# Sample attention with its partitions ordered (batch, quarter, token), and its transfers on SyncE's queue

## The chip, the core and the metric

The kernel runs on one core of a Trainium2 chip. The metric is device time in microseconds (us) of one execution, the median of several runs. Before the change the median of three runs is 2064.51 us (2064.17 to 2070.43). One more execution was taken by the hardware profiler.

## What is computed

One layer of a decoder trunk, for a prompt of 256 tokens and for 8 sample sequences of 4 tokens that share the weights: 288 token columns in all, everything in fp32. Cut to what matters here:

```
h = RMSNorm(x)                                    # d_model 2048
qa,ka,va,za,ba,aa, qb,kb,vb, uc, ga,gb,gc = split(h @ w_in)
out_a = gated delta rule over qa,ka,va            # 8 heads, prompt in chunks
out_b = dilated attention over qb,kb,vb           # 3 groups x 4 heads x 128
oc    = multi-scale pooling of uc, then w_pool
merged = sigmoid(ga)*(out_a@w_br_a) + sigmoid(gb)*(out_b@w_br_b) + sigmoid(gc)*(oc@w_br_c)
x = x + RMSNorm(merged @ w_out)
x = x + RMSNorm(SwiGLU(RMSNorm(x)))

# dilated attention of one sample token, group g with (window, dilation) = (128,1), (512,4), (2048,16)
idx = q_idx - arange(window // dil + 1) * dil     # rows of cache_win{g+1} followed by the 4 new rows
s   = q . k[idx] / sqrt(128);  p = exp(s - max)   # the max and the sum run over all three groups
out_b = sum(p * v[idx]) / sum(p)
```

The sample group reads its old keys and values from `cache_win1` (8 x 128 rows), `cache_win2` (8 x 512) and `cache_win3` (8 x 1024). One row is a key and a value of 4 heads x 128 numbers, 2 KB each. The new keys and values are also outputs (`win*_prompt`, `win*_sample`), and the kept part of the caches is copied to `win*_sample`.

## The kernel before, in words

**The trunk.** All large matmuls run through one list of items (`run_items`, L229). A weight tile is 128 x 1024 numbers, 512 KB. `load` (L158) brings it into one of five `raw` buffers on SyncE's queue, called SP here (L169). `feed` (L172) turns it into two fp32r parts: ScalarE (ACT) casts it to `wh` (L180), VectorE (DVE) computes the rest `wl` (L184). There are three buffers of each, and `feed(3)` keeps three tiles ready. Then TensorE (PE) runs 24 matmuls for the tile, 128 x 128 times 128 x 288 (L253 to L255). A `raw` buffer is free for the next load when L184 has read it. After each weight tile, `step` (L282) lets the background generators go on; their rates say how many of their pieces go with one tile.

**Where the keys and values are born.** Nine items compute qb, kb and vb of the three groups. The last evacuation of each (`evac_qkv`, L955) transposes the result on PE, copies it to `nat` tiles (L979, L981), and stores these by DMA: prompt rows to `win*_prompt` (L986), sample rows to a scratch array `scr` in DRAM (L988) and to `win*_sample` (L991). The `nat` tiles, like most others, come from a ring of 98 slots that is used in turn, so a later user of a slot waits for the store that reads it.

**Sample attention** (`attn_sample`, L1077) runs as a generator at 4.4 pieces a weight tile, started after the second key item and drained when branch b begins (`attn_finish`, L1009). It uses no matmul for the scores. A cache row for all sequences at once is a tile `kr` of 128 partitions x 512 numbers, 256 KB. For groups 2 and 3 the 128 partitions are 8 sequences x 4 quarters of the window x 4 tokens, and the kernel before orders them (token, batch, quarter). Each token needs other rows of the cache, since the dilation is 4 or 16: `sources` (L1101) writes the cache row as a pattern with the 4 tokens `r` outermost, then the 32 pairs (b q) (L1104 to L1106). There are 32 such rows of group 2 and 16 of group 3, for keys and again for values: 96 loads at L1106. For group 1 the partitions are (batch, 16 pieces of the window), one dimension of 128, 8 rows for keys and 8 for values (L1111); there the four tokens are handled by four instructions for each head. The new rows come from `scr` (`by_t`, L1086, and L1112).

For each row and head DVE does one instruction of 128 x 128 (four for group 1): a product with the query and a sum for the scores (L1142), then in the second pass a multiply-add into the output (L1192). Between the passes the maximum over partitions goes through DRAM in small DMAs (L1155 to L1167), and at the end PE adds over partitions with the 0/1 matrices `sel1` and `sel0` (L1196).

**Order of the work.** All DMAs of sample attention and of `evac_qkv` are issued by GpSimd (POOL; `dq` and `self.dq`), whose instructions run in order: a load that waits for a free `kr` buffer holds what is behind it. There are five `kr` buffers (`KR`, L25). Four loads are issued at the start (L1132), and each row that is taken up issues one more before it (L1123), so the load of the fourth row ahead uses the buffer of the row just finished. The first sample instruction after a new weight tile is tied behind that tile's L184 (`paced`, L274). The compiler framework orders the instructions of each engine by a model of their times, within the dependencies of the program; only the cache copies (L165) keep the written order.

Of the kernel before, what the change touches and what calls it, by code (L numbers as in the profile page):

```python
# [9 lines left out]
F32 = mybir.dt.float32  # L10
# [7 lines left out]
NT, NP, NS = 288, 256, 32  # L18
# [6 lines left out]
KR = 5  # L25
EPS = 1e-6
SC = 128.0 ** -0.5
WIN = (128, 512, 1028)
# [11 lines left out]
def shape_constants():  # L40
    r = np.arange(128)
    t, i = r[:, None], r[None, :]
    same4 = t // 4 == i // 4
    d = {}
    d["ident"] = t == i
    d["U"] = t <= i
    d["V"] = t > i
    d["ones"] = np.ones((128, 128))
    d["Ub"] = (t <= i) & same4
    d["Vb"] = (t > i) & same4  # L50
    d["m32"] = (i // 32 == t // 32 + 1) & ((t // 32) % 2 == 0)
    d["m64"] = (t < 64) & (i >= 64)
    d["mS1"] = same4 & (t % 2 == 0) & (i == t + 1)
    d["mS2"] = same4 & (t % 4 < 2) & (i % 4 >= 2)
    d["blk"] = t // 32 == np.arange(4)[None]
    d["bm"] = (t % 32) // 4 == np.arange(8)[None]
    d["bsel"] = t // 4 == np.arange(32)[None]
    c = np.arange(32)[None]
    d["sel1"] = (t // 32 == c % 4) & ((t % 32) // 4 == c // 4)
    d["sel0"] = np.concatenate([(t // 16 == c // 4) & (c % 4 == tt) for tt in range(4)], axis=1)  # L60
    d["fold"] = t % 32 == i % 32
    d["gsel"] = t % 32 == np.arange(16)[None]
    s0 = t % 16
    m0 = np.zeros((128, 4, 9), bool)
    for tt in range(4):
        m0[:, tt, :8] = s0 * 8 + np.arange(8)[None] >= tt
        m0[:, tt, 8] = ((s0 % 4 == 0) & (s0 // 4 <= tt))[:, 0]
    d["mask0"] = np.where(m0, 0.0, -1e30).reshape(128, 36)
    mt = np.ones((128, 50), bool)
    mt[:, 48:] = t % 4 == 0  # L70
    d["maskt"] = np.where(mt, 0.0, -1e30)
    ic = np.zeros((4, 15))
    for gi, w in enumerate((2, 4, 8, 16)):
        ic[gi] = 1.0 / np.minimum(w, np.arange(15) + 1)
    d["icnt"] = np.broadcast_to(ic.reshape(1, 60), (128, 60))
    for qb, name in ((0, "mp0"), (1, "mp1")):
        parts = []
        for dil in DILS:
            for kb in range(qb + 1):
                dist = (qb * 128 + t) - (kb * 128 + i)  # L80
                ok = (dist >= 0) & (dist % dil == 0) & (dist <= 128 * dil)
                parts.append(np.where(ok, 0.0, -1e30))
        d[name] = np.concatenate(parts, axis=1)
    pack = lambda spec: np.ascontiguousarray(
        np.concatenate([np.asarray(d[n], np.float32) for n, _ in spec], axis=1))
    return pack(C_SPEC), pack(M_SPEC)


class Layer:
# [865 lines left out]
    def evac_qkv(self, kind, g):  # L955
        vT = []

        def evac(h, ps):
            nc = self.nc
            t = self.res.popleft()  # L960
            nc.scalar.copy(t, ps)
            if kind == 2:
                vT.append(t)
            else:
                (self.kT if kind == 1 else self.qT)[g, h] = t
            if h < 3:
                return
            src = vT if kind == 2 else [(self.kT if kind == 1 else self.qT)[g, j] for j in range(4)]
            for tb in ([2] if kind == 0 else [1, 2] if (kind == 1 and g == 0) else [0, 1, 2]):
                w = NS if tb == 2 else 128  # L970
                p = self.ps("knat")
                for j in range(4):
                    nc.tensor.transpose(p[:w, j * 128:j * 128 + 128], src[j][:, tb * 128:tb * 128 + w],
                                        self.c["ident"])
                for hp in range(2):
                    n = self.U(name="nat")
                    cs = slice(hp * 256, hp * 256 + 256)
                    if hp == 0:
                        nc.scalar.copy(n[:w, :256], p[:w, cs])  # L979
                    else:  # L980
                        nc.vector.tensor_copy(n[:w, :256], p[:w, cs])  # L981
                    if tb < 2:
                        if not (g == 0 and tb == 0):
                            o = self.o[f"win{g + 1}_prompt"][0, 0].rearrange("r k h d -> r k (h d)")
                            r0 = 0 if g == 0 else tb * 128
                            self.dq.dma_start(o[r0:r0 + 128, kind - 1, cs], n[:, :256])  # L986
                    else:
                        self.dq.dma_start(self.scr[kind, g][:, cs], n[:NS, :256])  # L988
                        if kind > 0:
                            o = self.o[f"win{g + 1}_sample"][0].rearrange("b r k h d -> b r k (h d)")  # L990
                            self.dq.dma_start(o[:, WIN[g] - 4:, kind - 1, cs], n[:NS, :256])  # L991
                    if kind == 2 and tb < 2:
                        self.vn[g, tb, hp] = n
                    else:
                        self.free(n)
            self.free(*vT)
        evac.res = 4
        return evac
# [78 lines left out]
    def attn_sample(self, pool):  # L1077
        nc, c, a, scr = self.nc, self.c, self.a, self.scr
        dq = nc.gpsimd
        qt = pool.tile([128, 2, 512], F32, name="qt")  # L1080
        big = pool.tile([128, 4, 512], F32, name="big")
# [4 lines left out]
        def by_t(dst, kind, g):  # L1086
            src = scr[kind, g].rearrange("(b t) d -> t b d", t=4)
            for t in range(4):
                dq.dma_start(dst[t * 32:t * 32 + 32], src[t][:, None, :].to_broadcast([8, 4, 512]))

        for g in (1, 2):
            by_t(qt[:, g - 1], 0, g)
        q0s = scr[0, 0].rearrange("(b t) d -> t b d", t=4)
        for t in range(4):
            dq.dma_start(big[:, t], q0s[t][:, None, :].to_broadcast([8, 16, 512]))
        cw = [a["cache_win1"][0], a["cache_win2"][0], a["cache_win3"][0]]

        def row():
# [2 lines left out]
        def sources(kv):  # L1101

            for g, dil, n in ((1, 4, 32), (2, 16, 16)):
                src = cw[g].rearrange("b (q m r) k h d -> m k r (b q) (h d)", q=4, r=dil)  # L1104
                for m in range(n):
                    yield g, (m if g == 1 else 32 + m), lambda kr, s=src[m, kv][:4]: dq.dma_start(kr, s)  # L1106
            for g in (1, 2):
                yield g, 47 + g, lambda kr, g=g: by_t(kr, 1 + kv, g)
            src = cw[0].rearrange("b (s m) k h d -> m k (b s) (h d)", m=8)
            for m in range(8):  # L1110
                yield 0, m, lambda kr, s=src[m, kv]: dq.dma_start(kr, s)  # L1111
            yield 0, 8, lambda kr: dq.dma_start(kr, scr[1 + kv, 0][:, None, :].to_broadcast([32, 4, 512]))  # L1112

        todo = deque((kv,) + r for kv in range(2) for r in sources(kv))
        got = deque()

        def load():
            kv, g, m, fill = todo.popleft()
            kr = row()
            fill(kr)  # L1120
            got.append((kv, g, m, kr))
# [7 lines left out]
                if not got:  # L1129
                    return  # L1130

        for _ in range(KR - 1):  # L1132
            load()
        yield 5

        for g, m, kr in rows(0):
            for h in range(4):
                hs = slice(h * 128, h * 128 + 128)
                for t in (range(4) if g == 0 else (0,)):
                    q = big[:, t, hs] if g == 0 else qt[:, g - 1, hs]  # L1140
# [7 lines left out]
        mt = pool.tile([128, 4], F32, name="mt")  # L1148
        m0 = pool.tile([128, 16], F32, name="m0")
        nc.vector.tensor_reduce(mt, sct, axis=AX, op=OP.max)  # L1150
        nc.vector.tensor_reduce(m0, sc0.rearrange("p t h m -> p (t h) m"), axis=AX, op=OP.max)
        dmt = self.dr.tile([32, 16], F32, name="dmt")
        dm0 = self.dr.tile([8, 16, 4, 4], F32, name="dm0")
        dmx = self.dr.tile([4, 8, 4], F32, name="dmx")
        dq.dma_start(dmt.rearrange("c (q h) -> (c q) h", h=4), mt)  # L1155
        dq.dma_start(dm0.rearrange("b s t h -> (b s) (t h)"), m0)
        gm = pool.tile([32, 80], F32, name="gm")
        dq.dma_start(gm[:, 0:16], dmt)
# [2 lines left out]
        yield 4  # L1161
        mx = pool.tile([32, 4], F32, name="mx")
        self.paced(nc.vector.tensor_reduce(mx, gm.rearrange("p (x h) -> p h x", h=4), axis=AX, op=OP.max))
        dq.dma_start(dmx.rearrange("t b h -> (t b) h"), mx)
        dq.dma_start(mt, dmx.rearrange("t b h -> (t b) h")[:, None, :].to_broadcast([32, 4, 4]))
        for t in range(4):
            dq.dma_start(m0[:, t * 4:t * 4 + 4], dmx[t][:, None, :].to_broadcast([8, 16, 4]))  # L1167
        yield 4
        self.paced(nc.vector.tensor_tensor(sct, sct, mt[:, :, None].to_broadcast([128, 4, 50]), op=OP.subtract))
        s0 = sc0.rearrange("p t h m -> p (t h) m")  # L1170
# [9 lines left out]
        for g, m, kr in rows(1):  # L1180
            for h in range(4):
                hs = slice(h * 128, h * 128 + 128)
                for t in (range(4) if g == 0 else (0,)):
                    dst = o0[:, t, hs] if g == 0 else ot[:, hs]
# [336 lines left out]
```

## Time and profile before

| What | Value |
|---|---|
| median of 3 runs | 2064.51 us |
| the profiled execution | 2068.37 us, its span in the profile 2066.6 us |
| PE busy | 2010.6 us, 97% of the span, 15212 matmuls |
| DVE busy | 1324.2 us, 64% |
| ACT busy | 893.8 us, 43% |
| POOL busy | 291.6 us, 14% |
| moved by DMA | 425.50 MB: SP's queue (q1) 384.72 MB, POOL's (q0) 37.73 MB |
| sample attention's scores | DVE instructions from 451.4 to 742.9 us |
| sample attention's values | DVE instructions from 775.9 to 1051.3 us |

How to read it: PE's busy time is the union of modelled matmul times, so the idle time is what counts. A row `A <- B: total, times, longest` in the view of waits says how long A's engine sat idle until B released it. In the view by stretches of time each engine has its busy time with its instructions in brackets, then come the clock granted to PE (1.00 is full speed), the mean busy share of the 16 DMA engines, and the GB/s moved. The DMA share counts a packet from its start to its end, its waits on the way included. "DMA to landing" is the time from the issue of a transfer until its last byte is reported.

### The profile page before, as it was taken

The page shows a single profiled execution, that of the slowest core. Times are in us where ns is not written, and L with a number is a line of the kernel's source. Part 1 is how long each engine was busy: PE and PEld are TensorE (multiplying, and loading weights), DVE is VectorE, ACT ScalarE, POOL GpSimd, SP SyncE. Part 2 cuts the span into 40 slices and gives each one's busy share as a digit, 9 for nine tenths or more (in the row PEclk, how much of TensorE's full clock was granted, in tenths as well). Part 3 has the DMA queues.
Part 4 walks back from the last instruction along what each step waited for, and adds up shares of the span by engine and source line. Part 5 has one row for each costly group of instructions (what it writes and reads, how often), then busy time and mean ns, then how long its engine had stood idle before and what let it go on. Part 6 is the DMA issues. An engine that isn't in the chain of part 4 may idle for free. (4 is left out here: it accounts for less than half of the span.)

```text
span 2066.6 us, 38707 instructions
## 1 busy us (share of the span) xinstructions
PE 2010.6 (97%) x15212; PEld 1984.4 (96%) x15212; DVE 1324.2 (64%) x2857; ACT 893.8 (43%) x1414; POOL 291.6 (14%) x504
## 2 busy tenths in 40 slices
PE   8999999999799999989999989999999999999998
PEld 8989998999799999989999989999999999999997
DVE  7969558567688779878875475543554445454555
ACT  6654473453344444333334454334333333333344
POOL 2326312523320022322000000000000000000001
PEclk9999999999999999999999989999999999999999
DMA  8565546959995668998677646766767767677662
GB/s 268 160 182 169 176 140 197 228 173 238 219 205 183 181 184 198 226 220 245 195 229 234 218 160 212 226 222 217 225 216 228 230 217 226 218 225 227 217 205 97
DMA packets 240310, 425.50 MB, mean 206 GB/s; under 512 B 42736, under 2 KB 83200, under 8 KB 238464
## 3 DMA queue, kind: packets, MB, share of 16 engines
q1 hardware_dynamic: 207712, 384.72, 63.1%
q0 software_dynamic: 32272, 37.73, 8.0%
q8 instruction: 119, 1.95, 0.4%
q10 hardware_dynamic: 144, 0.59, 0.1%
q14 instruction: 63, 0.52, 0.1%
HBM read 410.44 MB, written 66.63 MB: 231 GB/s over the span
## 5 line engine op out<-in xcount | busy, mean ns | idle before, releaser
L184 DVE TENSOR_TENSOR wl<-raw,wh 128x1024 fp32r<-128x1024 f32 x585 | 720.2, 1232 | 519.0 <-ACT wh L180 516.7
L180 ACT CAST wh<-raw 128x1024 fp32r<-128x1024 f32 x585 | 612.7, 1050 | 917.9 <-PE m L254 792.3
L253 PE MATMUL m<-hh,wh 128*128 128x288 f32 x1792 | 532.7, 299 | 4.2 <-ACT wh L180 3.7
L255 PE MATMUL m<-hh,wl 128*128 128x288 f32 x1792 | 524.0, 298 | 8.3 <-DVE wl L184 8.3
L254 PE MATMUL m<-hl,wh 128*128 128x288 f32 x1792 | 531.3, 298 | 0.0
L253 PE MATMUL m<-xgh,wh 128*128 128x288 f32 x1408 | 415.8, 297 | 4.0 <-ACT xgh L373 4.0
L254 PE MATMUL m<-xgl,wh 128*128 128x288 f32 x1408 | 415.8, 296 | 3.2 <-DVE xgl L374 3.2
L255 PE MATMUL m<-xgh,wl 128*128 128x288 f32 x1408 | 414.6, 296 | 0.0
L255 PEld LDWEIGHTS m<-hh,wl 128*128 128x128 f32 x1792 | 335.1, 189 | 13.1 <-DVE wl L184 10.7
L253 PEld LDWEIGHTS m<-hh,wh 128*128 128x128 f32 x1792 | 337.7, 189 | 7.8 <-ACT wh L180 4.2
L254 PEld LDWEIGHTS m<-hl,wh 128*128 128x128 f32 x1792 | 338.2, 189 | 1.9 <-issue 1.8
L253 PEld LDWEIGHTS m<-xgh,wh 128*128 128x128 f32 x1408 | 265.5, 189 | 4.6 <-ACT xgh L373 4.3
L254 PEld LDWEIGHTS m<-xgl,wh 128*128 128x128 f32 x1408 | 266.4, 189 | 3.6 <-DVE xgl L374 3.5
L255 PEld LDWEIGHTS m<-xgh,wl 128*128 128x128 f32 x1408 | 265.4, 189 | 0.0
L253 PE MATMUL m<-hidh,wh 128*128 128x288 f32 x704 | 207.5, 295 | 0.0
L254 PE MATMUL m<-hidl,wh 128*128 128x288 f32 x704 | 207.2, 295 | 0.0
L255 PE MATMUL m<-hidh,wl 128*128 128x288 f32 x704 | 206.5, 295 | 0.0
L1449 POOL TENSOR_TENSOR yo<-y,xr 128x288 f32<-128x288 f32 x7 | 5.6, 821 | 1060.7 <-DVE y L1440 1060.7
L254 PEld LDWEIGHTS m<-hidl,wh 128*128 128x128 f32 x704 | 132.4, 188 | 0.0
L253 PEld LDWEIGHTS m<-hidh,wh 128*128 128x128 f32 x704 | 132.2, 188 | 0.0
L255 PEld LDWEIGHTS m<-hidh,wl 128*128 128x128 f32 x704 | 131.9, 188 | 0.0
L1106 POOL DMA_DIRECT2D kr<-cache_win x96 | 65.4, 682 | 250.0 <-DVE junk L1142 136.9
(386 smaller groups left out, 2704.4 us busy)
## 6 DMA issues: line engine op xcount, KB each, us to landing
raw<-w_in SPq DMA_DIRECT2D x247, 512.0 KB, 4.5
raw<-w_gu SPq DMA_DIRECT2D x176, 512.0 KB, 4.0
raw<-w_down SPq DMA_DIRECT2D x88, 512.0 KB, 4.9
win_sample<-cache_win SPq DMA_DIRECT2D x64, 512.0 KB, 5.4
kr<-cache_win POOLq DMA_DIRECT2D x112, 256.0 KB, 10.7
raw<-w_out SPq DMA_DIRECT2D x32, 512.0 KB, 5.0
win_sample<-cache_win SPq DMA_DIRECT2D x32, 508.0 KB, 5.2
st<-state_gdn SPq DMA_DIRECT2D x64, 128.0 KB, 3.2
```

The costliest lines, as they stand in the source:

```text
L180: i = nc.scalar.copy(wh, raw)
L184: self.last_wl = nc.vector.tensor_tensor(wl, raw, wh.bitcast(F32), op=OP.subtract)
L253: nc.tensor.matmul(out, lhsT=wh[:, c], rhs=xh, start=k == 0, stop=False)
L254: nc.tensor.matmul(out, lhsT=wh[:, c], rhs=xl, start=False, stop=False)
L255: nc.tensor.matmul(out, lhsT=wl[:, c], rhs=xh, start=False, stop=k == nk - 1)
L1106: yield g, (m if g == 1 else 32 + m), lambda kr, s=src[m, kv][:4]: dq.dma_start(kr, s)
L1449: (nc.vector if how == "v" else nc.gpsimd).tensor_tensor(out[:, d % 2], y, x, op=OP.add)
```

## The change

1. Partitions of groups 2 and 3 are ordered (batch, quarter, token). The pattern of a cache row becomes (b q) outermost with 32, then the 4 tokens; the stored constants `sel1` and `maskt` follow, and a DMA for one token writes every fourth partition (`t:128:4`) where it wrote a block of 32.
2. `evac_qkv`'s stores, `by_t`, the queries and all rows are issued by SyncE.
3. `KR - 2` loads are issued at the start, so that rows are loaded three ahead; there are still five buffers.
4. In the exchange of the maximum, the DRAM array is ordered (batch, token), and one DMA for `mt` becomes four.

```diff
-    d["sel1"] = (t // 32 == c % 4) & ((t % 32) // 4 == c // 4)
+    d["sel1"] = (t // 16 == c // 4) & (t % 4 == c % 4)
...
-    mt[:, 48:] = t % 4 == 0
+    mt[:, 48:] = (t // 4) % 4 == 0
@@ evac_qkv @@
-                            self.dq.dma_start(o[r0:r0 + 128, kind - 1, cs], n[:, :256])
+                            nc.sync.dma_start(o[r0:r0 + 128, kind - 1, cs], n[:, :256])
...
-                        self.dq.dma_start(self.scr[kind, g][:, cs], n[:NS, :256])
+                        nc.sync.dma_start(self.scr[kind, g][:, cs], n[:NS, :256])
...
-                            self.dq.dma_start(o[:, WIN[g] - 4:, kind - 1, cs], n[:NS, :256])
+                            nc.sync.dma_start(o[:, WIN[g] - 4:, kind - 1, cs], n[:NS, :256])
@@ attn_sample @@
-                dq.dma_start(dst[t * 32:t * 32 + 32], src[t][:, None, :].to_broadcast([8, 4, 512]))
+                nc.sync.dma_start(dst[t:128:4], src[t][:, None, :].to_broadcast([8, 4, 512]))
...
-            dq.dma_start(big[:, t], q0s[t][:, None, :].to_broadcast([8, 16, 512]))
+            nc.sync.dma_start(big[:, t], q0s[t][:, None, :].to_broadcast([8, 16, 512]))
...
-                src = cw[g].rearrange("b (q m r) k h d -> m k r (b q) (h d)", q=4, r=dil)
+                src = cw[g].rearrange("b (q m r) k h d -> m k (b q) r (h d)", q=4, r=dil)
                 for m in range(n):
-                    yield g, (m if g == 1 else 32 + m), lambda kr, s=src[m, kv][:4]: dq.dma_start(kr, s)
+                    yield g, (m if g == 1 else 32 + m), lambda kr, s=src[m, kv][:, :4]: nc.sync.dma_start(kr, s)
...
-                yield 0, m, lambda kr, s=src[m, kv]: dq.dma_start(kr, s)
-            yield 0, 8, lambda kr: dq.dma_start(kr, scr[1 + kv, 0][:, None, :].to_broadcast([32, 4, 512]))
+                yield 0, m, lambda kr, s=src[m, kv]: nc.sync.dma_start(kr, s)
+            yield 0, 8, lambda kr: nc.sync.dma_start(kr, scr[1 + kv, 0][:, None, :].to_broadcast([32, 4, 512]))
...
-        for _ in range(KR - 1):
+        for _ in range(KR - 2):
             load()
...
-        dmx = self.dr.tile([4, 8, 4], F32, name="dmx")
-        dq.dma_start(dmt.rearrange("c (q h) -> (c q) h", h=4), mt)
+        dmx = self.dr.tile([8, 4, 4], F32, name="dmx")
+        dq.dma_start(dmt.rearrange("(t b) (q h) -> b q t h", t=4, h=4), mt)
...
-        dq.dma_start(dmx.rearrange("t b h -> (t b) h"), mx)
-        dq.dma_start(mt, dmx.rearrange("t b h -> (t b) h")[:, None, :].to_broadcast([32, 4, 4]))
+        dq.dma_start(dmx.rearrange("b t h -> t b h"), mx)
         for t in range(4):
-            dq.dma_start(m0[:, t * 4:t * 4 + 4], dmx[t][:, None, :].to_broadcast([8, 16, 4]))
+            dq.dma_start(mt[t:128:4], dmx[:, t][:, None, :].to_broadcast([8, 4, 4]))
+            dq.dma_start(m0[:, t * 4:t * 4 + 4], dmx[:, t][:, None, :].to_broadcast([8, 16, 4]))
```

## The prediction, made before the changed kernel was run

> **What bounds the kernel now.** I read the page, then PE's busy time by stages of sample attention, then PE's waits in the stages that have idle time, then the transfers there.
>
> ```profile
> PE 2010.6 (97%) x15212; PEld 1984.4 (96%) x15212; DVE 1324.2 (64%) x2857; ACT 893.8 (43%) x1414; POOL 291.6 (14%) x504
> ```
>
> PE is the bound: a change of the transfers can only win back idle time of PE, or add some. The stages follow the DVE instructions that use the rows: group 2 and 3 rows of keys, group 1 rows of keys, the exchange of the maximum, then the same for values. The columns are the stretch, its length, five engines, PE's clock, the DMA share and GB/s.
>
> ```profile
> 450.00:628.00 178.00, 164.97 (x1231) 162.85 (x1230) 131.22 (x497) 71.31 (x109) 55.47 (x91) 0.98 0.99 225
> 628.00:743.00 115.00, 115.00 (x871) 114.69 (x870) 93.25 (x354) 48.24 (x65) 7.66 (x17) 1.00 0.59 175
> 743.00:775.00 32.00, 30.33 (x229) 30.10 (x228) 21.01 (x48) 14.57 (x21) 12.64 (x29) 1.00 0.65 182
> 775.00:951.00 176.00, 165.49 (x1217) 162.88 (x1216) 146.24 (x308) 65.75 (x84) 51.09 (x78) 0.99 1.00 222
> 951.00:1052.00 101.00, 101.00 (x766) 101.00 (x766) 89.39 (x183) 37.45 (x45) 6.91 (x9) 1.00 0.71 217
> ```
>
> Where the rows have the token outermost (first and fourth stretch), PE stands idle for 13.0 and 10.5 us, its clock drops, and the DMA share is 0.99 and 1.00. Where the rows are group 1's, PE never stands. PE's waits, first for 450 to 750 us, then for 750 to 960 us:
>
> ```profile
> PE pv L1065 <- ACT pT L1057: 6.8, 1, 6.8
> PE m L255 <- DVE wl L184: 3.2, 4, 1.1
> PE m L253 <- ACT wh L180: 2.0, 1, 2.0
> ```
> ```profile
> PE m L255 <- DVE wl L184: 9.5, 6, 2.8
> PE m L253 <- ACT wh L180: 1.7, 1, 1.7
> ```
>
> PE waits for the two halves of a weight tile, and once for ACT's copy of attention weights that stands behind another instruction. Both are downstream of transfers. The landing times of the `raw` weight loads, 512 KB each, in four stretches: 500 to 600, 600 to 750, 800 to 950, 950 to 1050 us.
>
> ```profile
> DMA to landing us min/median/max: 6.7/10.4/14.0
> ```
> ```profile
> DMA to landing us min/median/max: 3.4/4.1/12.3
> ```
> ```profile
> DMA to landing us min/median/max: 5.1/11.4/15.9
> ```
> ```profile
> DMA to landing us min/median/max: 3.5/3.9/5.9
> ```
>
> Weights land 2.5 to 3 times later beside the token-outermost rows. The rows themselves, 256 KB each from the same POOL queue, L1106 (token outermost) and L1111 (group 1):
>
> ```profile
> L1106 POOL DMA_DIRECT2D kr<-cache_win x96: 677/677/718, 392.0 to 932.7; - x96
> ...
> DMA to landing us min/median/max: 5.1/11.6/20.9
> ```
> ```profile
> L1111 POOL DMA_DIRECT2D kr<-cache_win x16: 536/538/576, 618.3 to 984.8; - x16
> ...
> DMA to landing us min/median/max: 3.0/4.6/7.2
> ```
>
> The same bytes take 11.6 us against 4.6. Volume alone doesn't do it, as two other stretches show: more or as many GB/s at a lower share.
>
> ```profile
> 0.00:50.00 50.00, 44.45 (x332) 42.99 (x333) 36.25 (x69) 32.04 (x53) 13.87 (x35) 1.00 0.83 273
> 100.00:400.00 300.00, 292.44 (x2364) 280.59 (x2363) 213.43 (x532) 152.60 (x362) 113.94 (x183) 1.00 0.64 181
> 1300.00:1600.00 300.00, 300.00 (x2266) 300.00 (x2265) 143.77 (x171) 118.25 (x147) 0.00 (x0) 1.00 0.70 223
> ```
>
> From the last row also the time of a weight tile: 2266 matmuls are 94.4 tiles of 24, so 3.18 us each.
>
> **The change, part by part.**
>
> *The row pattern.* It removes the token-outermost loads. Its value is bounded above by all of PE's idle time in the two stretches, 13.0 + 10.5 = 23.5 us, and the lost clock, 0.02 x 178 + 0.01 x 176 = 5.3 us: 28.8 us. Below, it is zero if the shape is not the cause. I take the upper end as the base, since in 628 to 743 and 951 to 1052 us the same weights, the same 4.4 DVE pieces a tile and group 1's rows give no idle time. That the shape, not the number of rows (1.1 a tile against 0.28), makes the difference is inferred. The Trainium skill (DMA: Bandwidth & Descriptors, "Why a DMA increments its semaphore by 16 and not by 1") says that a DMA runs on the largest number of engines up to 16 that divides the slowest dimension of both its sides; by it the old row used 4 engines and the new one uses 16, as group 1's rows do. The landings above agree with that; which engines worked, no row shows.
>
> *The queue.* Rows and stores leave POOL, where they stand behind each other:
>
> ```profile
> 529.85 0.51 POOL L988 DMA_DIRECT2D scr<-nat  x1 [4.28 <-DMA kr<-cache_win]
> ...
> 565.47 0.51 POOL L988 DMA_DIRECT2D scr<-nat  x1 [5.57 <-DMA kr<-cache_win]
> ```
> ```profile
> ACT oah L146 <- DMA win_sample<-nat: 17.9, 2, 9.2
> ```
>
> A store held back 4 to 6 us by row loads keeps a `nat` slot, and ACT, in order, waits 17.9 us in two pieces for it, with the weight casts behind it; PE's 6.8 and 2.0 us follow. On SP the stores wait for their own data only, so these two go. They are inside the 28.8.
>
> SP gets 192 more DMAs in 660 us (112 rows, 30 of `scr` and queries, 50 stores). Its cost for one, and its waits now:
>
> ```profile
> L169 SPq DMA_DIRECT2D raw<-w_in x132: 367/368/385, 451.1 to 1035.1; - x132
> ```
> ```profile
> L934 SPq DMA_DIRECT2D st<-state_gdn x32: 368/419/1499, 134.2 to 332.1; - x32
> ```
> ```profile
> SPq L169 <- DVE wl L184: 736.6, 287, 20.3
> ```
>
> At 0.42 us that is 81 us of issue. I cost it at nothing: SP mostly waits for a `raw` buffer to come free. The cover is the weights' lead:
>
> ```profile
> L184 DVE TENSOR_TENSOR wl<-raw,wh 128x1024 fp32r<-128x1024 f32 x585 | 720.2, 1232 | 519.0 <-ACT wh L180 516.7
> L180 ACT CAST wh<-raw 128x1024 fp32r<-128x1024 f32 x585 | 612.7, 1050 | 917.9 <-PE m L254 792.3 <-issue 53.8 <-DMA raw<-w_in 22.0
> ```
>
> Five buffers are 15.9 us from a free buffer to the `wl` that needs the new tile; less 1.05 for the cast, 1.23 for `wl` and 4.1 for landing, 9.5 us of slack. Beyond it each us that SP is held is a us of PE.
>
> *New waits on SP.* A row waits for DVE to finish an older row, a store for ACT's or DVE's `nat`, a `scr` row for the store before it; weight loads stand behind them. The nearest case is 300 to 400 us, where SP mixes weight loads with state loads, stores and a DRAM round trip:
>
> ```profile
> SPq L943 <- DVE X L743: 9.4, 11, 1.1
> ...
> SPq L747 <- DVE X L743: 2.0, 1, 2.0
> ```
>
> Nothing but weights waits longer than 2.0 us there, far below 9.5. Yet that mixed stage (100 to 400 us) leaves PE idle 7.6 of 300 us, 2.5%; over the two stretches, 354 us, that would be 8.9 us. The stages without idle time give 0. I take the middle, 4.5 us, as what remains.
>
> *Three ahead.* A load now uses the buffer of the last row but one, so it seldom waits at SP's head; the lead falls from four rows to three, 3 x 178 / 50 = 10.7 us against a landing of 4.6. Nothing. If rows still took 11.6, DVE would wait about 1 us a row.
>
> *The exchange and constants.* Three more POOL DMAs delay it by 1.9 us:
>
> ```profile
> L1167 POOL DMA_DIRECT2D m<-dmx x4: 622/633/637, 760.5 to 762.3; - x4
> ```
>
> It lies in a stage where the generator pauses and PE has tiles ready: 0, at most 1.9. The masks keep their sizes: 0.
>
> **Sum.** 28.8 - 4.5 = 24.3 us less. Against the profiled execution, 2068.4 - 24.3 = 2044.1; that execution lies 3.9 above the median of 2064.5, so the median should be 2040.2. About 0.3% (6.2 us) can be told from no change.
>
> **Rivals.** *Traffic, not shape.* Weights and rows together hold the DMA engines at 1.00, and the same bytes from SP do so again; only the two store waits go. That gives back 6.8 + 2.0 us and the first stretch's clock, 3.6: 2064.5 - 12.4 = 2052, up to 2060 with stores behind loads. The Trainium skill speaks for this one (same page, "Issuing engines are not separate DMA queues"): all queues run on the same 16 engines, and another queue saves only issue time. Against it: 273 GB/s at 0.83 and 223 at 0.70.
>
> *Nothing gained.* Rows land no faster, stores wait on SP as on POOL, or DVE takes over as the bound: 2064.5. DVE would be busy 146.2 of 163.7 us (89%) and 131.2 of 161.4 (81%) once the idle time is gone; the clean stretches have 89.4 of 101 (89%) and 93.3 of 115 (81%), which speaks against DVE.
>
> *Slower: a row at SP's head holds the weights.* POOL's waits in 628 to 743 us, where a row has 16 DVE instructions and lasts 115 / 9 = 12.8 us:
>
> ```profile
> POOL kr L1106 <- DVE junk L1142: 45.7, 4, 13.0
> POOL kr L1111 <- DVE junk L1142: 36.5, 4, 14.0
> ```
>
> If SP is held for 14.0 us, 4.5 beyond the slack, PE loses that; from six such rows on (27 us) the gain is gone, and with all 18 of group 1 (81 us) the time is 2040 + 81 = 2121. Against it: three ahead takes a whole row of 12.8 us from the wait, and both loads are released by DVE in DVE's own order, so a queue sorted by readiness holds nothing back. For it: the order is made from a model of times, which the chip need not follow.
>
> **How the numbers follow.** Forecast 0.64 (2032 to 2050), traffic 0.13 (2052 to 2060), nothing 0.08 (2064), slower 0.15. Faster by over 0.3% (under 2058.3): 0.64 and 0.10 of traffic, 0.74; within 0.3%: 0.03 of traffic and 0.07 of nothing, 0.10; slower: 0.15 and 0.01, 0.16. The range goes from 2032 (nearly the whole 28.8 and the 1.7 idle in the exchange) to 2065, past no change; the slower cases are left out above.
>
> **What would show it.** Right: DMA share of the two stretches at 0.75 or less, raw and row landings of 4 to 6 us there, PE idle under 5 us in each, no wait of ACT for `win_sample`, SP's waits at L1106 under 9.5 us. Wrong: SP waiting at a row while `raw` buffers are free, PE waiting for L180 or L184 in 628 to 743 us, or landings still near 10 us.

## The result, and the profile after

The changed kernel takes 2033.97 us (median of 4 runs, 2032.17 to 2035.02) against 2064.34 us before (4 runs): a ratio of 0.985 (95% interval 0.9823 to 0.9877), 30.4 us less. The forecast was 24.3 us less. The profiled execution took 2035.02 us, its span is 2033.2 us.

First the page's busy times of the changed kernel, in the form of the first line of the prediction.

```profile
PE 2002.3 (98%) x15212; PEld 1979.3 (97%) x15212; DVE 1329.1 (65%) x2857; ACT 894.6 (44%) x1414; POOL 168.7 (8%) x315
```

The same 15212 matmuls keep PE busy for 8.3 us less (2010.6 before), and the span is 33.4 us shorter. So PE's idle time fell by 25.1 us, from 56.0 to 30.9 us, and the other 8.3 us are shorter busy time. The mean granted clock of the two executions is 0.992 before and 0.995 after; 2010.6 us shrink by some 6 us between the two, an estimate. DVE has the work that it had. POOL lost 189 instructions, from which no gain was expected.

Now the stages, by the same DVE instructions as in the prediction; the two token-outermost stages of before have become 160 us long each.

```profile
450.00:610.00 160.00, 160.00 (x1222) 159.49 (x1221) 131.91 (x498) 71.65 (x109) 0.00 (x0) 1.00 0.78 248
610.00:725.00 115.00, 115.00 (x871) 114.69 (x870) 93.06 (x353) 48.42 (x65) 2.32 (x8) 1.00 0.59 175
725.00:755.00 30.00, 30.00 (x228) 30.00 (x227) 20.90 (x46) 14.03 (x21) 16.09 (x27) 1.00 0.61 183
755.00:915.00 160.00, 158.78 (x1194) 157.98 (x1193) 147.03 (x309) 64.33 (x82) 17.03 (x27) 1.00 0.78 246
915.00:1018.00 103.00, 103.00 (x781) 103.00 (x780) 89.97 (x183) 38.99 (x45) 3.13 (x4) 1.00 0.69 211
```

Read the second column against the first: PE is idle for 0, 0, 0, 1.2 and 0 us, where it was 13.0, 0, 1.7, 10.5 and 0. The clock is at 1.00 in all of them. Look also at the last two columns of the first and the fourth row: the DMA share has fallen from 0.99 and 1.00 to 0.78, while the rate has *risen* from 225 and 222 to 248 and 246 GB/s. The share is not a measure of how much is moved; it is how long packets are under way.

PE's waits from 440 to 750 us are gone altogether: the view has no row. From 750 to 960 us it has these three:

```profile
PE m L255 <- DVE wl L184: 0.7, 1, 0.7
PE m L1278 <- DVE ocl L1285: 0.3, 1, 0.3
PE m L253 <- DVE xp L1235: 0.2, 1, 0.2
```

ACT's wait for the stores, which was 17.9 us, from 450 to 650 us:

```profile
ACT oah L146 <- DMA win_sample<-nat: 2.7, 2, 1.9
```

And the loads of rows, now on SP, with their issue time in ns (least, median, most), and then the waits of SP's own queue at that line from 380 to 1060 us:

```profile
L1106 SPq DMA_DIRECT2D kr<-cache_win x96: 534/547/1557, 391.0 to 898.5; - x96
```
```profile
SPq L1106 <- DVE junk L1142: 39.4, 43, 2.6
SPq L1106 <- DVE ot L1192: 34.0, 38, 1.6
...
SPq L1106 <- DVE pll L147: 5.0, 1, 5.0
```

No single wait at a row is longer than 5.0 us, so none uses up the 9.5 us of slack. The trace of the changed kernel gives no landing times for transfers of SP, so whether rows land sooner has to be read from a kernel that leaves them on POOL; that is the first experiment.

### The profile page after: what moved, and what is told of

Its sections match the earlier page's. It is cut to its first block, busy times and chain, and to the rows that moved or that the text cites. A ratio compares the mean times of both kernels' runs of the same rounds, so it can differ in the third digit from the quotient of the medians.

```text
span 2033.2 us, 38677 instructions
## 1 busy us (share of the span) xinstructions
PE 2002.3 (98%) x15212; PEld 1979.3 (97%) x15212; DVE 1329.1 (65%) x2857; ACT 894.6 (44%) x1414; POOL 168.7 (8%) x315
## 5 line engine op out<-in xcount | busy, mean ns | idle before, releaser
L255 PEld LDWEIGHTS m<-hidh,wl 128*128 128x128 f32 x704 | 131.9, 188 | 0.0
L254 PE MATMUL m<-mgl,wh 128*128 128x288 f32 x256 | 75.1, 295 | 0.0
```

Of the source, the lines that this page charges most:

```text
L254: nc.tensor.matmul(out, lhsT=wh[:, c], rhs=xl, start=False, stop=False)
L255: nc.tensor.matmul(out, lhsT=wl[:, c], rhs=xh, start=False, stop=k == nk - 1)
```

## The experiments

The theory: the pattern of a row decides. With the token outermost (4 x 32 x 512) a row load is slow and delays what flies beside it; with 32 pairs outermost it isn't. The rivals: traffic (the volume of rows and weights together fills the DMA engines, and only the queue's order matters), and the queue (stores and rows no longer stand behind each other on POOL).

**1. The pattern alone.** The new partition order everywhere, with the exchange that goes with it; stores, queries and rows stay on POOL, four loads ahead. Each diff below is cut to the lines that matter; here the stores, the queries and the other rows go back to POOL in the same way.

```diff
-  lambda kr, s=src[m, kv][:, :4]: nc.sync.dma_start(kr, s)
+  lambda kr, s=src[m, kv][:, :4]: dq.dma_start(kr, s)
...
-        for _ in range(KR - 2):
+        for _ in range(KR - 1):
```

> The new order of partitions alone: pattern (b q) outermost, masks and exchange with it; all rows, queries and stores stay on POOL, four rows ahead. If the shape of the row loads was the cause: rows land in 4 to 6 us instead of 11.6, weights in 4 to 5 us in both stages, DMA share 0.8 or less, the waits of ACT for win_sample mostly gone because the stores no longer stand behind slow rows; 2036 to 2046 us. If the queue was the cause: rows still near 10 us, DMA share near 1.0, 2060 to 2066 us.

Measured: 2038.62 us (2038.18 to 2039.98), ratio 0.9877 (0.986 to 0.9893). The stages, and the row loads on POOL:

```profile
450.00:610.00 160.00, 160.00 (x1222) 159.49 (x1222) 131.71 (x495) 71.40 (x108) 48.63 (x90) 1.00 0.80 249
...
755.00:915.00 160.00, 158.80 (x1194) 157.99 (x1193) 147.46 (x307) 64.53 (x83) 45.74 (x81) 1.00 0.78 248
```
```profile
L1106 POOL DMA_DIRECT2D kr<-cache_win x96: 536/538/702, 390.8 to 899.9; - x96
...
DMA to landing us min/median/max: 2.9/3.9/9.5
```

Same queue, same bytes, same line: a row lands in 3.9 us where it took 11.6. The `raw` weights beside them, from 500 to 600 and from 800 to 950 us:

```profile
DMA to landing us min/median/max: 3.5/4.5/5.2
```
```profile
DMA to landing us min/median/max: 3.5/4.6/7.3
```

They took 10.4 and 11.4 us. PE's two stretches are as clean as in the full change, and ACT has no wait for a store in 450 to 650 us, although stores and rows still share POOL's queue. So the move to SP is not needed for any of this.

The slow rows reached PE by two roads before the change, which the landings alone don't show. In 450 to 628 us no weight cast of ACT waits for a weight transfer, though weights land 10.4 us after their issue in the median: that is 6.3 us more than the 4.1 of the clean stretch, and less than the 9.5 us of slack. What PE lost there came with ACT's 17.9 us of waiting for stores and DVE's 15.0 us of waiting for rows; the trace doesn't part the two. In 775 to 951 us weights take up to 15.9 us, and the casts do wait for them (ACT's waits in the kernel before):

```profile
ACT wh L180 <- DMA raw<-w_in: 17.7, 7, 3.3
ACT wh L180 <- DMA raw<-w_br_c: 9.9, 4, 3.4
```

In run 1 ACT waits neither for stores nor for weights in its two stretches. The 4.6 us that are left to the full change lie elsewhere; they are looked for below (runs 6 to 8).

**2. The queue alone.** The old partition order, with the constants and the exchange that go with it; rows, queries and stores on SP, three ahead.

```diff
-  src = cw[g].rearrange("b (q m r) k h d -> m k (b q) r (h d)", q=4, r=dil)
+  src = cw[g].rearrange("b (q m r) k h d -> m k r (b q) (h d)", q=4, r=dil)
...
-  lambda kr, s=src[m, kv][:, :4]: nc.sync.dma_start(kr, s)
+  lambda kr, s=src[m, kv][:4]: nc.sync.dma_start(kr, s)
```

> The queue alone: rows, queries and stores on SP, three rows ahead, but partitions in the old order with the token outermost. If the shape was the cause: weights and rows land no faster than before (10 us or more) in both stages; since weights and rows now stand in the same rings it can be worse than before, 2055 to 2130 us. If the queue was the cause: 2032 to 2040 us, rows at 4 to 6 us.

Measured: 2144.57 us (2142.13 to 2147.2), ratio 1.0393 (1.0371 to 1.0415): 80 us *slower* than before, and 14 us above the upper end of what was expected for this case. From the view of stretches, one of the scores and one of the values, and the sum of the table, which covers 380 to 1150 us:

```profile
450.00:620.00 170.00, 136.09 (x944) 132.08 (x943) 98.53 (x371) 56.34 (x93) 0.00 (x0) 0.90 0.59 177
...
915.00:1040.00 125.00, 97.61 (x676) 93.42 (x675) 83.28 (x166) 31.83 (x36) 9.69 (x12) 0.96 0.60 190
...
sum 770.00, PE 689.33 PEld 673.99 DVE 526.75 ACT 280.88 POOL 40.68; mean PE 114.89 PEld 112.33 DVE 87.79 ACT 46.81 POOL 6.78
```

PE is idle for 80.7 of 770 us. The DMA share is only 0.59, far from the 0.99 before, and still transfers are late: DVE alone waits 91.6 us for rows. The timeline of SP shows where the weights are held (start, duration, instruction):

```profile
568.00 2.47 SPq L169 DMA_DIRECT2D raw<-w_in  x1
570.56 1.17 SPq L1106 DMA_DIRECT2D kr<-cache_win  x1
571.83 2.80 SPq L169 DMA_DIRECT2D raw<-w_in  x1
574.72 1.26 SPq L1106 DMA_DIRECT2D kr<-cache_win  x1
576.07 1.19 SPq L169 DMA_DIRECT2D raw<-w_in  x1
577.35 4.14 SPq L1106 DMA_DIRECT2D kr<-cache_win  x1
581.58 2.59 SPq L169 DMA_DIRECT2D raw<-w_in  x1
584.27 1.26 SPq L1106 DMA_DIRECT2D kr<-cache_win  x1
585.62 2.99 SPq L169 DMA_DIRECT2D raw<-w_in  x1
```

Add a start and its duration: the next instruction starts 0.1 us later each time. In this cut SP does nothing but issue, and an issue of a weight tile, which took 0.37 us before, takes 1.2 to 3.0 us, that of a row up to 4.1 us. From the first of the five weight tiles to the start of the fifth it is 17.6 us, 4.4 us a tile, and PE uses one up in 3.18. Over the whole stretch from 450 to 620 us the issue instructions take 121.5 of 170 us, where in the change they take 65.7 of 160. So the queue of the weights itself runs late, and in this cut not because it stands idle for a `raw` buffer. This is the slower rival's place and its price, by another mechanism: not a row that waits for its buffer, but issue instructions that don't end. What holds them the trace doesn't say. The Trainium skill (DMA: Bandwidth & Descriptors, "Why a DMA increments its semaphore by 16 and not by 1") says that a DMA on fewer than 16 engines takes the lowest-numbered ones when SP issues it, and a moving set when POOL does. By that rule all old rows on SP load the same four engines, which agrees with 0.59 of share beside late transfers, and with POOL being the milder place; which engines worked, no row shows.

**3. The stores alone on SP.** The kernel before, with only the three stores of `evac_qkv` moved; one is shown.

```diff
-                        self.dq.dma_start(self.scr[kind, g][:, cs], n[:NS, :256])
+                        nc.sync.dma_start(self.scr[kind, g][:, cs], n[:NS, :256])
```

> The kernel before with only the stores of new keys and values on SP. By the prediction's sum the two waits for stores go (8.8 us of PE and 3.6 us of clock): about 2052 us, rows still at 11 us, the stage of values unchanged (PE idle about 10 us). If the stores are only a symptom of slow transfers: the wait moves to another place and the time stays at 2058 to 2066.

Measured: 2064.63 us (2059.08 to 2073.08), ratio 1.0005 (0.9988 to 1.0023). ACT's waits from 450 to 650 us:

```profile
ACT oah L146 <- DMA win_sample<-nat: 9.8, 1, 9.8
...
ACT oah L146 <- DMA scr<-nat: 7.7, 1, 7.7
```

That is 17.5 us, where it was 17.9. The stores no longer stand behind row loads, and they are as late as ever. Standing in POOL's queue was not what held ACT. Together with run 1, where the same stores on POOL hold nobody beside rows of the new pattern, this puts it on the old rows in flight.

**4. The old order, one DMA for each token, on SP.** A row is fetched by four DMAs of 32 x 512, each with the 32 pairs outermost. The bytes, their places in DRAM and in the partitions are those of run 2; what differs is the outermost count, and that a row is four DMAs of 64 KB.

```diff
-  lambda kr, s=src[m, kv][:4]: nc.sync.dma_start(kr, s)
+  lambda kr, s=src[m, kv]: [nc.sync.dma_start(kr[t * 32:t * 32 + 32], s[t]) for t in range(4)]
```

> As the queue alone, old order of partitions, but each row of groups 2 and 3 as four DMAs, one a token, each with the 32 pairs (b q) outermost to 32 neighbouring partitions. Same bytes, same places, 288 more DMAs on SP. If the number of items in the outermost dimension decides: rows land in 4 to 6 us, DMA share under 0.85, 2032 to 2042 us. If instead the neighbourhood of the cache rows in DRAM decides (tokens next to each other): as slow as the queue alone.

Measured: 2045.98 us (2043.66 to 2050.69), ratio 0.9914 (0.9892 to 0.9936).

```profile
450.00:620.00 170.00, 163.29 (x1210) 161.82 (x1209) 129.52 (x491) 69.98 (x108) 0.00 (x0) 0.97 0.80 231
760.00:915.00 155.00, 152.01 (x1141) 151.00 (x1140) 141.88 (x293) 63.48 (x81) 18.01 (x27) 1.00 0.80 233
```
```profile
L1106 SPq DMA_DIRECT2D kr<-cache_win x384: 310/413/1682, 393.2 to 919.2; - x192
```

Four times as many DMAs on the weights' queue, and 99 us less than run 2: a median issue is back at 0.41 us, and PE's idle time in 450 to 620 us falls from 33.9 to 6.7 us. So the gain doesn't need the four tokens' rows next to each other in DRAM; an outermost count of 32 is enough for most of it. The time is 4 us above the expected range.

The outermost count can be read in the packets of SP's queue (the first number; from the page of the change, of run 2 and of run 4):

```profile
q1 hardware_dynamic: 229856, 420.84, 66.6%
q1 hardware_dynamic: 228704, 420.83, 63.8%
q1 hardware_dynamic: 234464, 420.86, 67.2%
```

Run 2 has 1152 packets fewer than the change, 12 for each of its 96 old rows. Run 4 has 4608 more, 16 for each of its 288 additional DMAs. In the trace all of these are packets of 4 bytes; the packets with data are equal in number and size. So a DMA with 32 outermost has 16 small packets and an old row only 4. They are the same 16 and 4 that the prediction worked with for the engines; which engines worked is still not shown.

The 12 us that run 4 stays behind the change include this pair of waits, which the change doesn't have (380 to 1150 us):

```profile
PE knat L973 <- ACT ev L961: 6.7, 2, 3.5
```

**5. Four rows ahead.** The changed kernel with its fourth load back.

```diff
-        for _ in range(KR - 2):
+        for _ in range(KR - 1):
```

> The changed kernel with four rows ahead as before (KR - 1), so that a row load on SP uses the buffer of the row just finished. If SP's order follows readiness, as the state stage suggested, nothing changes: 2032 to 2036 us, the weights' lead kept. If three ahead is what keeps rows from holding the weights: SP waits at L1106 grow beyond the slack of 9.5 us and the time rises, to 2045 or more.

Measured: 2035.08 us (2033.05 to 2035.56), ratio 0.9862 (0.9846 to 0.9877): no different from the change. SP's waits at a row's line with four ahead:

```profile
SPq L1106 <- DVE junk L1142: 38.7, 43, 2.6
SPq L1106 <- DVE ot L1192: 34.0, 38, 1.6
```

They have the lengths that they have with three ahead, so that edit does nothing here.

**6. New pattern, stores on SP, rows on POOL.**

```diff
-  lambda kr, s=src[m, kv][:, :4]: nc.sync.dma_start(kr, s)
+  lambda kr, s=src[m, kv][:, :4]: dq.dma_start(kr, s)
...
-        for _ in range(KR - 2):
+        for _ in range(KR - 1):
```

> New order of partitions, stores of new keys and values on SP, rows and queries on POOL with four ahead. The pattern alone took 2038.6 us and the whole change 2034.0; but in their profiles the compute ends at 2028.5 and 2029.3 us, and the 4.7 us between lie behind it, where POOL's last instructions start late. If that tail and not the rows' queue makes the difference, this kernel gives 2033 to 2035 us with a short tail or 2038 to 2039 with a long one, PE's idle time the same in both; if rows on POOL cost time, PE shows new idle time in the two stretches.

Measured: 2036.39 us (2034.89 to 2039.05), ratio 0.9872 (0.9858 to 0.9886), between run 1 and the change, with PE as clean. So what SP brings at all is the few us of run 1. Where are they? The last row of the chain that ended last, and the page's span, of run 1 and then of the changed kernel:

```profile
2028.12 0.40 ACT yo L1447
```
```profile
span 2037.1 us, 38713 instructions
```
```profile
2028.87 0.40 ACT yo L1447
```
```profile
span 2033.2 us, 38677 instructions
```

Run 1 ends its compute 0.75 us *earlier*, and then takes 8.6 us to the end of the span where the change takes 3.9. All of the difference lies behind the last computation, where no row is loaded any more. In run 6 that end is 5.7 us, and before the change it is 3.9. Over all profiles it is 5.7 to 8.6 us where POOL issues rows of the new pattern (runs 1, 6, 7, 9 and 10) and 3.7 to 4.1 us everywhere else.

**7. Fewer instructions on POOL.** To see whether the long end comes from the number of DMAs on POOL: run 1 with the four `mt` loads of the exchange on SP, which leaves POOL about as many as before.

```diff
-            dq.dma_start(mt[t:128:4], dmx[:, t][:, None, :].to_broadcast([8, 4, 4]))
+            nc.sync.dma_start(mt[t:128:4], dmx[:, t][:, None, :].to_broadcast([8, 4, 4]))
```

> The pattern alone, but the four small DMAs for mt in the exchange go on SP, so that POOL has four instructions fewer, as many as in the kernel before. If the late end of POOL in the pattern alone comes from its number of instructions: the tail is short again, 2033 to 2035 us. If it comes from rows on POOL's queue: the tail stays, 2038 to 2039 us.

Measured: 2040.24 us (2039.43 to 2041.57), ratio 0.989 (0.9877 to 0.9903); the end is 8.2 us. So the number of POOL's instructions is not the cause.

**8. More instructions on POOL.** The kernel before, with eight small instructions of POOL at the start.

```diff
+        pad = self.cp.tile([128, 1], F32, name="pad8")
+        for _ in range(8):
+            nc.gpsimd.memset(pad, 0.0)
```

> The kernel before with eight small memsets more on POOL, at its very start. If the number of POOL's instructions makes the late end: 4 to 5 us behind the last compute, about 2069 us. If not: as the kernel before, 2064 to 2066 us.

Measured: 2058.12 us (2052.61 to 2060.58), ratio 0.9972 (0.9955 to 0.9988). The end is 3.9 us, so more instructions don't make it long either. The run was a miss in another way: it is 0.3% *faster* than before, and no gain was expected. PE's idle time in the two stretches of before:

```profile
450.00:628.00 178.00, 170.17 (x1266) 168.80 (x1265) 134.91 (x513) 75.79 (x116) 56.69 (x93) 0.97 0.95 231
775.00:951.00 176.00, 168.82 (x1251) 165.98 (x1250) 151.59 (x318) 67.16 (x85) 55.38 (x82) 1.00 0.99 232
```

It is 7.8 and 7.2 us, where it was 13.0 and 10.5. The old rows did less damage in this execution; that the eight instructions shift when rows and weights meet is a guess that no run tests. A difference of 0.3% between two versions with the old pattern says little about the edit. Why POOL ends late behind rows of the new pattern stays open.

**9. Every row twice, at the wrong place.** Run 1, and each row of groups 2 and 3 is fetched again into an array in DRAM that nothing reads: the new pattern with more volume, against the traffic rival.

```diff
             fill(kr)
+            if g and m < 48:
+                fill(self.dr.tile([128, 512], F32, name="kx", bufs=4))
```

> The pattern alone, and each row of groups 2 and 3 is fetched a second time, by the same pattern, into a DRAM array that nothing reads: 96 more transfers of 256 KB on POOL, 25 MB more. If volume was not the cause and the shape was: PE still has little idle time in the two stretches, though about 60 to 70 GB/s more are moved; 2038 to 2048 us. If volume decides: the idle time of the kernel before comes back, 2055 us or more. If the late end grows with POOL's DMAs: 10 us or more behind the last compute.

Measured: 2082.39 us (2080.89 to 2083.57), ratio 1.0087 (1.006 to 1.0113). It missed its aim:

```profile
L1106 POOL DMA_DIRECT2D kx<-cache_win x96: 524/524/987, 3.7 to 146.6; - x96
```

Bound to nothing, the second fetches were ordered to the first 147 us, ahead of other instructions of POOL, and the row loads began at 447.6 us where they begin at 390.8 in run 1. The time says nothing on volume beside the rows. The end is 7.1 us, so 96 more DMAs on POOL don't lengthen it. Where a load lies has to be looked up before its run is read.

**10. Every row twice, in place.** The same, each second fetch held behind the newest `wl` of a weight tile.

```diff
-                fill(self.dr.tile([128, 512], F32, name="kx", bufs=4))
+                self.behind(fill(self.dr.tile([128, 512], F32, name="kx", bufs=4)), self.last_wl)
```

> The kernel with the new pattern on POOL's queue (2038.6 us), in which every group 2 and 3 row is fetched a second time, with the same new pattern, into an array in DRAM that nothing reads, and this time each second fetch is held behind the newest VectorE instruction of a weight tile (L184), so that it goes beside the rows and not at the start. It adds 96 x 256 KB = 25 MB in the two stretches of 160 us, some 75 GB/s on 247. Theory (the pattern decides, not the volume): the weights still land in under 9.5 us, TensorE idles less than 5 us in each of the two stretches, and the time is 2036 to 2048. Rival (traffic): the stretches are as full as before the change, the weights land in 10 us or more, TensorE idles 10 us or more in each, and the time is 2055 or more. If the second fetches come elsewhere again, the run says nothing.

Measured: 2039.72 us (2036.11 to 2040.99), ratio 0.9884 (0.9862 to 0.9906). Now they lie beside the rows:

```profile
L1106 POOL DMA_DIRECT2D kx<-cache_win x96: 522/536/907, 431.2 to 893.7; - x96
```
```profile
450.00:610.00 160.00, 160.00 (x1224) 159.41 (x1223) 130.89 (x496) 71.77 (x110) 74.60 (x137) 1.00 0.93 321
...
755.00:915.00 160.00, 158.39 (x1190) 157.59 (x1190) 148.25 (x308) 65.81 (x86) 68.99 (x125) 1.00 0.91 318
```

Four tenths more than before the change (321 against 225 GB/s), at a share of 0.93, and PE is idle for 0 and 1.6 us. The weights' landings from 500 to 600 us:

```profile
DMA to landing us min/median/max: 4.2/6.2/8.7
```

Volume does delay them, from 4.5 to 6.2 us, and that is inside the slack. Before the change they took 10.4 us beside half the row bytes. Traffic is refuted as the cause, as far as volume goes: the second fetches end in DRAM and not in the partitions, as the first do. The end is 7.7 us here.

**11. The change again**, on the chip of run 9.

> The changed kernel once more, beside the others on one chip: 2032 to 2036 us, four microseconds behind the last compute.

Measured: 2034.42 us (2033.66 to 2038.64), ratio 0.9861 (0.9837 to 0.9884), which repeats the result. No run here beats the change.

## Why the prediction was right

The mechanism was the forecast one: the token-outermost rows were what made PE idle. Two terms were mis-sized, the lost clock (too small) and the idle time that remains (too large), and one step of the reasoning, on the stores, was wrong without touching the sum. Point by point:

*The base, 28.8 us.* It was right in kind and not a bound. Of the 23.5 us of idle time in the two stretches 22.3 are gone, and the 1.7 us of the exchange too. But PE's busy time fell by 8.3 us, where the prediction counted 5.3 us of lost clock from two rounded columns (0.98 and 0.99). So the span fell by 33.4 us, more than the upper end.

*The 4.5 us that remain.* This term failed. It was the middle between the clean stages and the mixed stage at 100 to 400 us. The measured remainder is 1.2 us: stages with SP's new work are like the clean stages, not like the mixed one. The profiled execution, forecast at 2044.1, came at 2035.0; of the 9.1 us between, 3.0 are PE's busy time and 6.1 the idle time (25.1 in the whole span, against 23.5 - 4.5 = 19.0).

*The range.* Its lower end of 2032 was given as nearly the whole 28.8 and the 1.7 of the exchange, but 2064.5 - 30.5 is 2034.0. The measured 2033.97 us lies there, so that it fell inside the forecast case of 2032 to 2050 owes something to luck in how the end was drawn.

*Shape, not number of rows.* It was inferred, and runs 1, 4 and 10 show it: same queue and bytes with another outermost count, same addresses split by token, and twice the rows with the new count.

*The queue.* The prediction said of the two store waits that they go because stores on SP wait for their own data only. Run 3 shows that this step is wrong: on SP the stores cost ACT 17.5 us as before. Run 1 shows them gone on POOL. They hung on the rows in flight. The sum was not harmed only because these waits had been counted inside the 28.8, and that is luck.

*192 more DMAs on SP for nothing, under 9.5 us of slack.* It held for the new pattern: PE has one wait for `wl` left, 0.7 us. It would not have held for the old pattern: in run 2 the same moves cost 80 us. The edit has no price of its own; its price depends on the pattern of what is moved.

*New waits, three ahead, the exchange.* A wait at a row is at most 5.0 us, run 5 shows that, with the new pattern, three ahead changes nothing, and PE is not idle at all in 725 to 755 us, where the longer exchange lies.

*The signs that were named.* The landings (run 1) and PE's idle time came as named; the DMA share is 0.78 and not 0.75 or less, and ACT still waits 2.7 us for `win_sample`. Neither reaches PE.

*The rivals.* Traffic falls by run 10. DVE as the bound falls by its own numbers: 131.9 of 160 us and 147.0 of 160 us busy (92%), with 1.2 us of PE waiting for it in the second. The slower rival stood in the right place, SP's head, but in run 2 the queue ran late by issue instructions that stretch, not by a row that waits for its buffer; the new pattern keeps that from happening.

## What to carry to other kernels

Read the outermost count of every DMA that flies beside a critical stream: here 4 against 32 was worth about 26 us at equal bytes on the same queue (run 1), and the tokens' places in DRAM were not what mattered (run 4). On POOL it showed as a DMA share near 1.00 at a rate that another stretch moved at 0.70; on SP the share was 0.59, so the share alone is no sign of it. Repair the pattern before moving a transfer to the queue of the critical stream; the same move made the kernel 80 us slower with the old pattern and did no harm with the new one. When several edits come together, run each alone: here one brought nearly all of the gain, one nothing, and one harm by itself.

## What the runs showed of the hardware that was not expected

- Issue instructions stretch: with the old rows on SP an issue of a row lasts 1.19 us in the median and up to 4.14 us, and those of weight tiles up to 4.25 us, while the mean DMA share is 0.59 to 0.64 in the stages of sample attention. The rows' shape held up SP's queue while the engines were on average far from full. What holds an issue was not found.
- On POOL the issue itself is longer with the old pattern: 677 ns for each of 96 rows, 538 ns with the new one, for equal bytes.
- A row with 32 outermost leaves 16 packets of 4 bytes on SP's queue, one with 4 outermost leaves 4 (runs 2 and 4 against the change). The packet counts of a page so show the shape of the transfers on that queue; on POOL's queue the packets of 4 bytes are as many with the old rows (3536 before, 3584 in run 1 with three more DMAs).
- Packets under 512 bytes are 42736 before, 24400 in run 1, and 22096 in run 2. The old pattern has the fewest of the three on SP, where it is slowest; small packets are not what makes it slow.
- The span goes on for 8.6 us after the last computation in run 1 and for 3.9 in the change. The runs tie it to rows of the new pattern issued by POOL, about 1100 us before; its cause was not found.
